# A third stream in prompt attention: the samples' paged-cache attention in units of 1024 tokens

## The chip, the cores and the metric

The kernel runs on one core of a Trainium2 chip. A core has a matrix engine (TensorE, in the profile PE, its weight loads PEld), a vector engine (VectorE, DVE), an activation engine (ScalarE, ACT), a general engine (GpSimd, POOL) and a sync engine (SyncE, SP) that issues most of the DMAs; GpSimd issues the gathers from the paged cache. Each engine works through its own queue in order and waits on semaphores. The metric is the device time of one execution in microseconds, as the median of several runs.

## The reference

One step of a two-layer decoder: a gated delta-rule mixer, a feed-forward part, latent attention, a feed-forward part again. It serves one prompt of 16 + 1024 tokens and 8 samples of one new token each, which all pass through the same matrices as 1048 columns. The change lies in the latent attention of the second layer. For a sample, with 8 heads, it is

```
q     = (rmsnorm(h @ w_q_a) @ w_q_b)            # per head: 128 plain, 64 rotary
q_lat = q_plain . w_uk                           # 256 latent numbers per head
s     = (q_lat . c_past + rope(q_pe) . k_past) * scale     # 4096 cached tokens
p     = softmax([s, s_new])                      # s_new: the token itself
o     = (p @ [c_past, c_new]) @ w_uv             # 128 per head
out   = concat(o) @ w_out
```

`c_past` (256 numbers a token) and `k_past` (64) lie in pages of 128 tokens, in an order that a page table gives. The prompt's 1040 tokens attend to one another causally; their keys and values are made from the latent with `w_uk` and `w_uv`. All arithmetic is float32.

## The kernel before

Tensors are kept with channels on partitions and tokens as columns, in three chunks (280, 384, 384); the samples are the first 8 columns of the first chunk. A float32 product is made of three products of rounded halves (`mm3`, lines 226 to 229), so most lines of the profile read L227, L228, L229 and are told apart by their tiles. Some products stay plain float32, which TensorE makes in two passes; a trace counts both.

`merge` (line 834) is what sets the order: it takes several generators, each of which yields a position before its next piece, and always runs the one whose position is lowest. A scheduler behind the kernel then orders each engine's queue by those priorities and by its own view of when operands are ready. The attention part of the second layer is three stages.

- Prompt attention, lines 1226 to 1441. `attend` goes through 8 heads of 9 query blocks: scores (`sc`, lines 1348 to 1384), softmax, the weights turned (`ptr`, `pT`) and multiplied with the values (`po`). `heads_in` makes queries (`qps`), keys (`knps`), rotary queries and values (`vps`) of the next head, just under a head earlier. Here also the samples' queries of the head are carried to the latent (`ukt`, `pq`). All of these but the scores use two PSUM buffers, `mtile` (line 98); a PSUM tile is free again when ScalarE or VectorE has copied it out.
- The samples' cache, `cache_unit` (line 1464): 16 units of 2048 tokens, two for a sample. GpSimd gathers two latent tiles (`cg`) and a rotary tile (`krt`). TensorE turns them (`dkt`, `dct`) through three PSUM buffers of their own; ScalarE and VectorE copy the result (`cT`, `krT`). The scores `dscr` are 8 x 4 products that each use 32 columns of the array, so four of them can run side by side. The value products `pv` are made in the same way.
- Beside the units, from position 0.05 to 1.0, the output projection of the prompt (`outp`, line 300, tile `psop`), without the samples' 8 columns; the units take positions 0 to CA = 0.4. `join` (line 1541) then merges the four key groups and the new token, carries the result through `w_uv` (`dov`) and makes the samples' own output projection (`dop`, line 1600; turned by `dopt`, line 1606), whose weights it loads a second time.

The lines of the latent scores:

```
for j in range(4):
    PE.matmul(sc[32 * j:32 * j + 32, :], ql[:, k, b, :], cT[:, j, :], start=(k == 0), stop=False,
              tile_position=(0, 32 * j))
```

Of the kernel before, what the change touches and what calls it, by code (L numbers as in the profile page):

```python
# [11 lines left out]
F32 = mybir.dt.float32  # L12
F32R = mybir.dt.float32r
# [7 lines left out]
P = 128  # L21
D = 1024
# [22 lines left out]
CA = 0.4  # L45
# [10 lines left out]
PTB = 4  # L56
# [5 lines left out]
def tile_step(ctx: ExitStack, tc: tile.TileContext, I, O, stop=None):  # L62
# [54 lines left out]
    # per-channel vectors as columns  # L117
# [56 lines left out]
    with tc.tile_pool(name="init", bufs=2, reuse_waits="tile") as ip, \  # L174
# [19 lines left out]
        # tokens to channel-major, normalised  # L194
# [40 lines left out]
    def stat(pp, aps, n, dst, dim):  # L235
        """dst[p, t] = (sum over channels / dim + eps)^-0.5 on every partition."""
# [10 lines left out]
    def boundary(pp, wide, c, wname, split=True, halves=False, store=False):  # L247
        """x <- x + acc * rstd * w for one chunk, kept in acc and, as halves, in xh and xl; the old x is in them or in x_d."""
# [99 lines left out]
    # ------------------------------------------------------------------ layer A mixer  # L348
# [38 lines left out]
    # previous conv rows of the samples, channel-major  # L387
# [9 lines left out]
    def gates():  # L397
# [20 lines left out]
        # a and b columns  # L418
# [40 lines left out]
        # cumulative decay  # L459
# [8 lines left out]
        # beta  # L468
# [91 lines left out]
    def chunks(h, p0, p1):  # L560
        """Everything of a head that does not need the running state."""
# [54 lines left out]
        # queries, meanwhile  # L616
# [21 lines left out]
        # last conv rows and sample rows  # L638
# [13 lines left out]
        # inverse of the 32-wide diagonal blocks by substitution: row k = 3 r + q of a block on partition (q, block)  # L652
# [81 lines left out]
    def recur(h, p0, p1):  # L734
        """The running state of a head, its outputs, and the samples."""
# [110 lines left out]
    def tail_a(p0, p1):  # L846
        """Out projection of the first heads while the last ones finish."""
# [14 lines left out]
    def tail_b(p0, p1):  # L862
        """The residual, channel-major."""
# [58 lines left out]
    # ------------------------------------------------------------------ gated conv feed-forward  # L922
# [170 lines left out]
    # ------------------------------------------------------------------ layer B: shared latent, attention  # L1093
# [8 lines left out]
    c_new = ukr.tile([NS, KVL], F32, name="c_new")  # L1102
    pgt = ukr.tile([P, NS], I32, name="pgt")
    for r in range(4):
        SP.dma_start(pgt[32 * r:32 * r + 32, :], I["page_table"].rearrange("b j -> j b"))
    rq = ukr.tile([P, 6], F32, name="rq")
    SP.dma_start(rq, I["c_rq"])
    idx = ukr.tile([P, 4, NS], I32, name="idx")
    idr = ukr.tile([P, 2, NS], I32, name="idr")
    for g in range(4):  # L1110
        V.tensor_scalar(idx[:, g, :], pgt, 16.0, rq[:, g:g + 1], op0=ALU.mult, op1=ALU.add)
    for g in range(2):
# [576 lines left out]
```

## Time and profile before

| | us |
|---|---|
| median of 3 runs | 3343.46 (3340.5 to 3355.22) |
| span of the profiled execution | 3338.6 |
| prompt attention, 1783 to 2173 | 390 |
| cache units beside the output projection, 2173 to 2412 | 239 |
| join beside the projection, 2412 to 2466 | 54 |
| rest of the projection, 2466 to 2514 | 48 |

The span runs from the first to the last instruction of one profiled execution; what its whole time was is not listed apart, and the median of the runs, taken without a profile, is 4.9 us above it. The page gives busy times by engine; since matmuls overlap one another, TensorE's real pace is read from the starts in the timeline. A wait is put down to what released it. Idle time of an engine counts only where TensorE or the end waits for it.

### The profile page before, as it was taken

How to read it: one execution, taken by the hardware profiler on the slowest of the kernel's cores; microseconds unless marked ns; L12 is line 12 of the kernel's file. 1: busy time of each engine (PE TensorE's matmuls, PEld its weight loads, DVE VectorE, ACT ScalarE, POOL GpSimd, SP SyncE). 2: the span in 40 equal slices, each digit the busy share in tenths (PEclk: the TensorE clock that was granted, in tenths of full speed). 3: DMA queues.
4: the chain of work that ended last, by engine and by line, in shares of the span. 5: the costliest groups of instructions: out<-in, count | busy, mean ns of one | idle time of the engine just before them, and what ended most of it. 6: DMA issues, size and time to landing. Idle time of an engine off the chain costs nothing.

```text
span 3338.6 us, 52527 instructions
## 1 busy us (share of the span) xinstructions
PE 3151.7 (94%) x20846; PEld 2874.7 (86%) x20846; DVE 2031.4 (61%) x4139; ACT 1255.9 (38%) x2541; POOL 860.2 (26%) x1013
## 2 busy tenths in 40 slices
PE   7999999999899999999888999999998999999997
PEld 6888888888699999999877888856677999999996
DVE  4877777766854555555666666544457455655556
ACT  4656555663432222222334444433224322222223
POOL 1432222210442223222431001112104323322322
PEclk9999999999899999999999999999999999999999
DMA  3222222236311111111121000255432111111111
GB/s 109 59 72 71 59 64 69 69 105 184 93 52 39 52 51 45 46 39 55 48 79 39 25 19 27 65 214 195 155 107 77 52 45 45 45 41 56 45 39 65
DMA packets 267649, 235.08 MB, mean 70 GB/s; under 512 B 57918, under 2 KB 246596, under 8 KB 263284
## 3 DMA queue, kind: packets, MB, share of 16 engines
q1 hardware_dynamic: 260224, 189.69, 19.7%
q0 software_dynamic: 6912, 41.95, 3.4%
q8 instruction: 164, 2.69, 0.3%
q14 instruction: 81, 0.66, 0.1%
q10 hardware_dynamic: 268, 0.09, 0.0%
HBM read 198.84 MB, written 33.40 MB: 70 GB/s over the span
## 4 chain that ended last, share of the span: by engine, by line
PE 77%; DVE 14%; DMA 3%; issue 3%; ACT 2%; POOL 1%; SPq 0%; ACTq 0%; DVEq 0%; POOLq 0%
PE fps L228 9%; PE fps L229 9%; PE fps L227 9%; PE fdn L228 5%; PE fdn L227 5%; PE fdn L229 5%; PE psu L227 2%; PE psu L229 2%; PE po L1409 2%; PE psu L228 2%; PE dscr L1494 2%; DVE acc L287 2%; DVE xs L660 1%; DVE tm L658 1%; PE psop L227 1%
## 5 line engine op out<-in xcount | busy, mean ns | idle before, releaser
L144 POOL TENSOR_TENSOR ws<-ws,vec 128x1024 f32<-128x1024 f32 (+1 forms) x127 | 247.6, 1950 | 433.4 <-DMA ws<-in_f_w_up_dram 173.2
L228 PE MATMUL fps<-xfl,wh 128*128 128x384 f32 (+1 forms) x1056 | 343.7, 326 | 8.3 <-POOL xfl L295 8.3
L227 PE MATMUL fps<-xfh,wh 128*128 128x384 f32 (+1 forms) x1056 | 341.7, 324 | 8.0 <-ACT xfh L293 7.0
L228 PE MATMUL fps<-xbl,wh 128*128 128x384 f32 (+1 forms) x1056 | 342.5, 324 | 6.1 <-POOL xbl L295 6.1
L229 PE MATMUL fps<-xfh,wl 128*128 128x384 f32 (+1 forms) x1056 | 342.4, 324 | 0.0
L227 PE MATMUL fps<-xbh,wh 128*128 128x384 f32 (+1 forms) x1056 | 340.6, 323 | 1.1 <-ACT xbh L293 0.5
L229 PE MATMUL fps<-xbh,wl 128*128 128x384 f32 (+1 forms) x1056 | 340.2, 322 | 0.0
L966 DVE TENSOR_TENSOR fu<-fps,RS 128x384 f32<-128x384 f32 x176 | 98.1, 557 | 386.7 <-PE fps L229 386.2
L151 ACT CAST wh<-ws 128x1024 fp32r<-128x1024 f32 (+1 forms) x144 | 148.0, 1028 | 488.1 <-PE fps L228 374.0
L227 PE MATMUL fdn<-gh,dh 128*128 128x384 f32 (+1 forms) x960 | 315.8, 329 | 0.0
L228 PE MATMUL fdn<-gl,dh 128*128 128x384 f32 (+1 forms) x960 | 311.9, 325 | 0.0
L229 PE MATMUL fdn<-gh,dl 128*128 128x384 f32 (+1 forms) x960 | 309.0, 322 | 0.0
L1044 DVE TENSOR_TENSOR acc<-acc,fdn 128x384 f32<-128x384 f32 (+1 forms) x432 | 216.9, 515 | 108.5 <-PE fdn L229 107.7
L227 PE MATMUL psu<-xah,wh 128*128 128x384 f32 (+1 forms) x768 | 261.2, 340 | 11.3 <-ACT u L533 7.0
L228 PE MATMUL psu<-xal,wh 128*128 128x384 f32 (+1 forms) x768 | 259.1, 337 | 0.4 <-DVE xal L223 0.4
L229 PE MATMUL psu<-xah,wl 128*128 128x384 f32 (+1 forms) x768 | 258.7, 337 | 0.7 <-DVE wl L152 0.7
L975 DVE SCALAR_TENSOR_TENSOR fy<-fu,fcv,fy 128x1064 f32<-128x1064 f32 x176 | 238.6, 1358 | 7.5 <-ACT fy L973 7.3
L152 DVE TENSOR_TENSOR wl<-ws,wh 128x1024 fp32r<-128x1024 f32 (+1 forms) x144 | 173.7, 1206 | 70.3 <-ACT wh L151 70.1
L228 PEld LDWEIGHTS fps<-xfl,wh 128*128 128x128 f32 x1056 | 200.8, 190 | 10.7 <-POOL xfl L295 10.5
L227 PEld LDWEIGHTS fps<-xfh,wh 128*128 128x128 f32 x1056 | 200.4, 190 | 9.4 <-ACT xfh L293 7.9
L228 PEld LDWEIGHTS fps<-xbl,wh 128*128 128x128 f32 x1056 | 199.6, 189 | 8.0 <-POOL xbl L295 7.7
L229 PEld LDWEIGHTS fps<-xfh,wl 128*128 128x128 f32 x1056 | 200.8, 190 | 0.4
(963 smaller groups left out, 7857.1 us busy)
## 6 DMA issues: line engine op xcount, KB each, us to landing
ws<-in_f_w_up_dram SPq DMA_DIRECT2D x88, 512.0 KB
ds<-in_f_w_down_dram SPq DMA_DIRECT2D x44, 512.0 KB
ws<-in_a_w_in_dram SPq DMA_DIRECT2D x32, 512.0 KB
xt<-in_x_prompt_dram SPq DMA_DIRECT2D x16, 512.0 KB
of<-og_d SPq DMA_DIRECT2D x32, 192.0 KB
xr<-x_d SPq DMA_DIRECT2D x16, 384.0 KB
GC<-gcd SPq DMA_DIRECT2D x24, 174.0 KB
Ss<-in_state_delta_S_dram SPq DMA_DIRECT2D x8, 512.0 KB
```

Source lines behind the costliest of these rows:

```text
L144: G.tensor_tensor(st, st, bc(fo, [P, kt, m]), op=ALU.mult)
L151: A.copy(hi, st)
L152: V.tensor_tensor(lo, st, hi, op=ALU.subtract)
L227: PE.matmul(ps, wh, ah, start=start, stop=False)
L228: PE.matmul(ps, wh, al, start=False, stop=False)
L229: PE.matmul(ps, wl, ah, start=False, stop=stop)
L287: V.scalar_tensor_tensor(a_[:, k + j, :], a_[:, k + j, :], vc(wname, k + j), res[j], op0=ALU.mult, op1=ALU.add)
L966: V.tensor_tensor(u[:, 18 + t0:18 + t0 + n], ps[:, :n], RS[:, t0:t0 + n], op=ALU.mult)
L975: V.scalar_tensor_tensor(y, u[:, j:j + LW], fcv[:, l, j, tl:tl + 1], y, op0=ALU.mult, op1=ALU.add)
L1044: V.tensor_tensor(acc[c][:, m, :], acc[c][:, m, :], ps[:, :n], op=ALU.add)
L1409: PE.matmul(po[:, :nq], vt[:kk, kb, P * (h % 2):P * (h % 2) + P], pT[:kk, j, :nq], start=(kb == 0), stop=(kb == i))
L1494: PE.matmul(sc[32 * j:32 * j + 32, :], ql[:, k, b, :], cT[:, j, :], start=(k == 0), stop=False, tile_position=(0, 32 * j))
```

## The change

The cache stage is gone as a stage. Prompt attention now has a third and a fourth stream, the samples' queries (`sample_queries`) and their cache (`cache_all`, positions 0.25 to 7.3 of the 8 heads). A unit is 1024 tokens: one latent gather, one rotary gather, half the columns in every product. Its transposes use the two buffers of `mtile`; its scores and value products share one PSUM bank, `halves`. The samples' queries are made for all heads at once from `w_q_b` in float32, no longer taken from the prompt's query tiles. Rings are shorter: softmax weights 2 for 3, their turned form 3 for 4, query tiles 2 for 3, rotary queries 3 for two heads for 4, values in three tiles of one head instead of two of two, the results `po` in one bank. The query norm takes the place of an earlier one (RQ = RS). After the join the samples' heads go to `og_d` beside the prompt's, and the output projection, now alone, takes all 1048 columns; `dop` and `dopt` are gone.

In the diff only the core is shown; of the old functions what is removed is in the listing above, of the new ones the main lines stand.

```diff
-PTB = 4
+PTB = 3
+PB = 2
+C0 = 0.25
+C1 = 7.3
...
-        opp = e2.enter_context(tc.tile_pool(name="ato", bufs=2, space=PSUM, reuse_waits="tile"))
+        opp = e2.enter_context(tc.tile_pool(name="ato", bufs=1, space=PSUM, reuse_waits="tile"))
+        dpp = e2.enter_context(tc.tile_pool(name="dps", bufs=1, space=PSUM, reuse_waits="tile"))
+        dc = e2.enter_context(tc.tile_pool(name="dc", bufs=1, reuse_waits="tile"))
+        cpg = e2.enter_context(tc.tile_pool(name="dcp", bufs=2, reuse_waits="tile"))
+        po4 = opp.tile([P, 4, C], F32, name="po")
+        halves = dpp.tile([P, 2, 256], F32, name="scpv")
...
-            return sp.tile([P, 384], F32, tag=nm, name=nm, bufs=3 if nm == "qu" else 2)
+            return sp.tile([P, 384], F32, tag=nm, name=nm, bufs=2 if nm == "qu" else 1)
...
-                pt = mtile("ukt")
-                for k in range(2):
-                    PE.transpose(pt[:, P * k:P * k + P], st[:, 3 + k, :], ident)
-                hd["ukT"] = sp.tile([P, 256], F32, tag="ukT", name="ukT", bufs=2)
-                A.copy(hd["ukT"], pt[:, :256])
...
-                        at[h + j]["qr"] = ap.tile([P, T], F32R, tag=f"qr{j}", name=f"qr{j}")
+                        at[h + j]["qr"] = ap.tile([P, T], F32R, tag="qr", name=f"qr{j}", bufs=3)
...
-                if c == 0:
-                    pq = mtile("pq")
-                    for k in range(2):
-                        PE.matmul(pq[:, NS * k:NS * k + NS], hd["ukT"][:, P * k:P * k + P], u[:, 0:NS], start=True, stop=True)
-                    V.tensor_copy(ql[:, :, :, h], pq[:, :2 * NS].rearrange("p (k s) -> p k s", k=2))
...
-                pp = sp.tile([C, NP], F32, tag="P", name="P")
+                pp = sp.tile([C, NP], F32, tag="P", name="P", bufs=PB)
...
-                        ot["po"] = opp.tile([P, C], F32, tag="o", name="po")
+                        ot["n"] = (ot.get("n", 0) + 1) % 4
+                        ot["po"] = po4[:, ot["n"], :]
...
-        cpg = e2.enter_context(tc.tile_pool(name="dcp", bufs=4, reuse_waits="tile"))
-        trp = e2.enter_context(tc.tile_pool(name="dtr", bufs=3, space=PSUM, reuse_waits="tile"))
...
+        def sample_queries():
+            yield -0.86
+            ps = halves[:, 0, :]
+            for a in range(2):
+                t = big("wq8")[:, :12 * P].rearrange("p (k h m) -> p k h m", k=3, h=4)
+                for k in range(3):
+                    SP.dma_start(t[:, k], wq[:, k, 4 * a:4 * a + 4, 0:128])
+                yield -0.6 + 0.1 * a
+                for h in range(4):
+                    o = NS * (4 * a + h)
+                    for k in range(3):
+                        PE.matmul(ps[:, o:o + NS], t[:, k, h, :], qa8[:, k, :], start=(k == 0), stop=(k == 2))
+            t = big("wr8")[:, :12 * P].rearrange("p (k m) -> p k m", k=3)
+            for k in range(3):
+                SP.dma_start(t[:, k, :].rearrange("p (h m) -> p h m", h=H), wq[:, k, :, 128:192])
+            yield -0.35
...
+            t = big("uk8").rearrange("p (k m) -> p k m", k=2)
+            SP.dma_start(t, I["kv_w_uk"].rearrange("(k p) h n -> p k (h n)", p=P))
...
+            pq = halves[:, 1, :]
+            for h in range(0, H, 4):
+                uT = cmat("ukT")
+                for i in range(2):
+                    yield -0.2 + 0.04 * (h + 2 * i)
+                    pt = mtile("ukt")
+                    for j in range(4):
+                        o = P * (h + 2 * i + j // 2)
+                        PE.transpose(pt[:, P * j:P * j + P], t[:, j % 2, o:o + P], ident)
...
+        def fetch(n):
+            if n < 4 * NS and n not in fetched:
+                b, g = divmod(n, 4)
+                cg = big("cg")
+                off = bass.IndirectOffsetOnAxis(ap=idx[:, g, b:b + 1], axis=0)
+                kr = cpg.tile([P, 8 * ROPE], F32, tag="kr", name="kr")
+                G.indirect_dma_start(kr, None, rrows, off)
+                G.indirect_dma_start(cg, None, crows, off)
+                fetched[n] = cg, kr
...
+        def cache_unit(n):
+            b, g = divmod(n, 4)
+            yield 0.0
+            fetch(n)
+            cg, kr = fetched.pop(n)
+            krT = cpg.tile([P, 512], F32, tag="krT", name="krT", bufs=1)
+            pt = mtile("dkt")
+            for i in range(4):
+                PE.transpose(pt[:, P * i:P * i + P], kr[:, P * i:P * i + P], ident)
+            A.copy(krT, pt)
+            cT = []
             for k in range(2):
...
+            yield 0.4
+            sc = halves[:, 0, :]
+            for k in range(2):
                 for j in range(4):
+                    PE.matmul(sc[32 * j:32 * j + 32, :], ql[:, k, b, :], cT[k][:, 2 * j:2 * j + 2, :], start=(k == 0), stop=False,
                               tile_position=(0, 32 * j))
...
+            yield 0.65
+            pT = cpg.tile([P, 2, P], F32, tag="dpT", name="dpT")
+            pt = mtile("dpt")
+            for c in range(2):
+                PE.transpose(pt[:, P * c:P * c + P], p[:, P * c:P * c + P], ident)
+            A.copy(pT, pt[:, :256].rearrange("p (a b) -> p a b", a=2))
+            yield 0.85
+            pv = halves[:, 1, :]
+            for c in range(2):
                 for j in range(4):
+                    o = KVL * key(j, c)
+                    PE.matmul(pv[32 * j:32 * j + 32, :], pT[:, c, 32 * j:32 * j + 32], cg[:, o:o + KVL],
+                              start=(c == 0), stop=(c == 1), tile_position=(0, 32 * j))
+            fetch(n + 2)
...
         def cache_all(p0, p1):
+            yield p0
+            fetch(0)
+            fetch(1)
+            for n in range(4 * NS):
+                for f in cache_unit(n):
+                    yield p0 + (p1 - p0) * (n + f) / (4 * NS)
+            yield p1 + 0.05
+            yield from join(p1 + 0.05, p1 + 0.5)
...
+                SP.dma_start(og_d[h][:, 0:NS], os_[:, h, :])
...
-            # their columns of the output projection
-                SP.dma_start(st, I["b_w_out"][0, P * h:P * h + P, :])
-                for i in range(2):
-                    PE.matmul(ps[i][:NS, :], os_[:, h, :], st[:, 512 * i:512 * i + 512], start=(h == 0), stop=(h == H - 1))
...
+        merge(attend(), *[heads_in(h, h - HA, h - HB) for h in range(H)], sample_queries(), cache_all(C0, C1))
+    emp.close()
...
-        merge(cache_all(0, CA), outp(I["b_w_out"][0], og_d, groups, ogp, 0.05, 1.0, True, NS, 6))
+        merge(outp(I["b_w_out"][0], og_d, groups, ogp, 0.0, 1.0, True, 0, 6))
```

Three places in TensorE's queue. First the scores of a cache unit before, in the middle of the stage; `dct` are turned keys, `dscr` the scores, and a wait names the engine waited for.

```order
L1488 MATMUL dct__23719<-ident,cg 128x128 [waits Activation_49]
L1488 MATMUL dct__23719<-ident,cg 128x128 x3
L1494 MATMUL dscr<-cT,ql 32x512
L1494 MATMUL dscr<-cT,ql 32x512 [waits DVE_49]
L1494 MATMUL dscr<-cT,ql 32x512 [waits Activation_49]
L1488 MATMUL dct__23730<-ident,cg 128x128 [waits PE_49]
L1494 MATMUL dscr<-cT,ql 32x512 [waits DVE_49]
L1488 MATMUL dct__23730<-ident,cg 128x128 x3
L1488 MATMUL dct__23736<-ident,cg 128x128 [waits PE_49]
L1488 MATMUL dct__23736<-ident,cg 128x128 x3
L1488 MATMUL dct__23742<-ident,cg 128x128 [waits PE_49]
```

The four products of the first latent half each wait for a copy of their own, and a transpose stands before the last one.

Now the same place of a unit after the change; the scores are written to `scpv`, `qps` are queries of the next head, `ptr` turned weights of the prompt's attention.

```order
L229 MATMUL qps<-qah,wh 128x280
L230 MATMUL qps<-qal,wh 128x280
L231 MATMUL qps<-qah,wl 128x280
L1546 MATMUL scpv<-cT,ql 32x256 x6
L1546 MATMUL scpv<-cT,ql 32x256 [waits DVE_49]
L1546 MATMUL scpv<-cT,ql 32x256
L1550 MATMUL scpv<-krT,qr_s 32x256 x4
L1390 MATMUL ptr<-ident,P 116x116 [waits PE_49]
L1390 MATMUL ptr<-ident,P 116x116
```

Six of the eight latent products stand together behind a group of queries; two more follow behind one wait, then the four rotary ones.

Last the start of attention after the change, in head 0: `wr` is the rotary query weights of the samples, `uk` the key weights that `ukt` turns, and the wait at the end is for the landing of a DMA.

```order
L1475 MATMUL scpv<-qa_17476,wr_18399 128x8 x9
L229 MATMUL sc<-knh,qnh 116x348 [waits Activation_49]
L230 MATMUL sc<-knl,qnh 116x348
L231 MATMUL sc<-knh,qnl 116x348 [waits Pool_49]
L1356 MATMUL sc<-kTh,qr_18272 116x348
L1357 MATMUL sc<-kTl,qr_18272 116x348
L229 MATMUL sc<-knh,qnh 116x464 [waits PE_49,Activation_49]
L230 MATMUL sc<-knl,qnh 116x464
L231 MATMUL sc<-knh,qnl 116x464
L1356 MATMUL sc<-kTh,qr_18272 116x464
L1357 MATMUL sc<-kTl,qr_18272 116x464
L1498 MATMUL ukt<-ident,uk_18465 128x128 [waits DMAHW0_49]
```

Between the last reading of the rotary weights and the first of the key weights stand ten score products of head 0. Nothing of this stood there before.

## Rows read from the trace of the kernel before

**Rows 1.** The page: span, and busy time of the engines

```profile
span 3338.6 us, 52527 instructions
PE 3151.7 (94%) x20846; PEld 2874.7 (86%) x20846; DVE 2031.4 (61%) x4139; ACT 1255.9 (38%) x2541; POOL 860.2 (26%) x1013
```

**Rows 2.** The page: the chain that ended last, by engine

```profile
PE 77%; DVE 14%; DMA 3%; issue 3%; ACT 2%; POOL 1%; SPq 0%; ACTq 0%; DVEq 0%; POOLq 0%
```

**Rows 3.** Stages: us; PE, PEld, DVE, ACT, POOL busy (x); clock; DMA share; GB/s

```profile
1783.00:2173.00 390.00, 373.37 (x2440) 313.46 (x2438) 238.65 (x662) 173.90 (x425) 41.95 (x42) 1.00 0.13 39
2173.00:2412.00 239.00, 234.70 (x1788) 142.16 (x1789) 108.53 (x222) 74.96 (x155) 39.84 (x42) 0.99 0.53 192
2412.00:2440.00 28.00, 28.00 (x190) 24.08 (x189) 11.41 (x41) 3.44 (x9) 0.10 (x1) 0.81 0.08 22
2440.00:2466.00 26.00, 23.93 (x78) 9.20 (x76) 7.82 (x12) 4.28 (x6) 2.12 (x3) 0.95 0.61 193
2466.00:2514.00 48.00, 45.46 (x280) 42.55 (x280) 36.08 (x59) 18.61 (x28) 3.80 (x2) 1.00 0.28 79
```

**Rows 4.** Timeline of a cache unit, TensorE: start, us, instructions

```profile
2326.39 1.93 PE L1517 MATMUL pv<-cg,dpT 128*32 128x256 f32 x32
2328.26 0.44 PE L1477 MATMUL dkt<-ident,krt 128*128 128x128 f32 x2
2328.53 0.60 PE L1488 MATMUL dct__23701<-ident,cg 128*128 128x128 f32 x4
2328.97 0.60 PE L1488 MATMUL dct__23707<-ident,cg 128*128 128x128 f32 x4
...
2330.58 1.35 PE L1494 MATMUL dscr<-cT,ql 128*32 128x512 f32 x6
2331.87 0.33 PE L1488 MATMUL dct__23730<-ident,cg 128*128 128x128 f32 x1
...
2333.10 0.55 PE L1488 MATMUL dct__23730<-ident,cg 128*128 128x128 f32 x3
...
2334.97 1.90 PE L1494 MATMUL dscr<-cT,ql 128*32 128x512 f32 x8
2336.80 1.06 PE L1498 MATMUL dscr<-krT,qr_s 64*32 64x512 f32 x8
2337.80 0.45 PE L227 MATMUL psop<-ogh,wx 128*128 128x384 f32 x1
...
2342.96 0.44 PE L1477 MATMUL dkt<-ident,krt 128*128 128x128 f32 x2
```

**Rows 5.** Groups by line, 2412 to 2466 us: output projection of the samples

```profile
L1600 PE MATMUL dop<-wos,os 128*8 128x512 f32 x32 | 16.6, 652 | 2.1 <-DMA wos<-in_b_w_out_dram 2.0
...
L1606 PE MATMUL dopt<-ident,ys 8*128 8x8 f32 x8 | 0.8, 207 | 0.0
```

**Rows 6.** Groups by line, 1783 to 2173 us: samples' latent queries

```profile
L1289 PE MATMUL pq<-qu,ukT 128*128 128x8 f32 x32 | 4.5, 249 | 0.5 <-DVE qu L1279 0.5
```

**Rows 7.** Gathers of latents (line 1469), then of rotary keys (line 1472)

```profile
DMA to landing us min/median/max: 5.5/7.0/8.8
...
DMA to landing us min/median/max: 6.0/7.9/8.9
```

**Rows 8.** Stages as rows 3, of an earlier layer and of attention's start

```profile
200.00:700.00 500.00, 459.29 (x3620) 423.51 (x3619) 372.38 (x1145) 295.18 (x819) 140.28 (x220) 0.97 0.26 69
1783.00:1830.00 47.00, 39.12 (x252) 33.63 (x251) 30.13 (x79) 22.49 (x57) 7.99 (x8) 1.00 0.18 53
```

**Rows 9.** Timeline of the same unit, copies of turned keys

```profile
2329.22 0.59 ACT L1492 COPY cT<-dct__23701 128x512 f32<-128x512 f32 x1 [2.88 <-PE dct__23701 L1488]
...
2329.60 0.69 DVE L1490 COPY cT<-dct__23707 128x512 f32<-128x512 f32 x1
```

**Rows 10.** Waits in attention: TensorE for copies, total us, times, longest

```profile
PEld vps L1325 <- ACT vt L1328: 8.4, 5, 1.8
...
PEld qps L227 <- DVE qu L1279: 3.4, 6, 1.0
```

More of the change, by code (lines that the diff above doesn't have):

```diff
@@ L44 @@
 PAGE = 128
-CA = 0.4
 CA0 = 0.65
@@ L1102, in tile_step @@
     c_new = ukr.tile([NS, KVL], F32, name="c_new")
+    qa8 = ukr.tile([P, 3, NS], F32, name="qa8")
     pgt = ukr.tile([P, NS], I32, name="pgt")
@@ L1105, in tile_step @@
         SP.dma_start(pgt[32 * r:32 * r + 32, :], I["page_table"].rearrange("b j -> j b"))
-    rq = ukr.tile([P, 6], F32, name="rq")
+    rq = ukr.tile([P, 4], F32, name="rq")
     SP.dma_start(rq, I["c_rq"])
     idx = ukr.tile([P, 4, NS], I32, name="idx")
-    idr = ukr.tile([P, 2, NS], I32, name="idr")
     for g in range(4):
         V.tensor_scalar(idx[:, g, :], pgt, 16.0, rq[:, g:g + 1], op0=ALU.mult, op1=ALU.add)
-    for g in range(2):
-        V.tensor_scalar(idr[:, g, :], pgt, 8.0, rq[:, 4 + g:5 + g], op0=ALU.mult, op1=ALU.add)
     emp = ExitStack()
@@ L1315, in v_weights @@
                 hd["uv"] = uh, ul
-                vt = ap.tile([C, NCK, 256], F32, tag="vt", name="vt")
-                at[h]["vt"] = at[h + 1]["vt"] = vt
+                for j in range(2):
+                    at[h + j]["vt"] = ap.tile([C, NCK, P], F32, tag="vt", name="vt", bufs=3)
             def vals(kb):
@@ new lines, in fetch, with key @@
+        def fetch(n):
[7 more added lines that the diff above has]
+                fetched[n] = cg, kr
+        def key(j, c):
+            return 4 * (j // 2) + 2 * c + j % 2
@@ new lines, in cache_unit @@
+        def cache_unit(n):
[9 more added lines that the diff above has]
+            cT = []
+            for k in range(2):
+                t = cmat("cT")
+                cT.append(t)
+                for hf in range(2):
+                    yield 0.06 + 0.12 * k + 0.06 * hf
+                    pt = mtile("dct")
+                    for i in range(4):
+                        o = KVL * key(2 * hf + i // 2, i % 2) + P * k
+                        PE.transpose(pt[:, P * i:P * i + P], cg[:, o:o + P], ident)
+                    (V.tensor_copy if hf else A.copy)(t[:, 4 * hf:4 * hf + 4, :], pt.rearrange("p (a b) -> p a b", a=4))
+            yield 0.4
+            sc = halves[:, 0, :]
+            for k in range(2):
@@ L1507, in cache_unit @@
             A.activation(p, sc, AF.Exp, bias=nb, scale=SCALE, accum_out=ls)
-            pT = sp.tile([P, 4, P], F32, tag="dpT", name="dpT")
-            pt = dtr("dpt")
-            for i in range(4):
-                PE.transpose(pt[:, P * i:P * i + P], p[:, P * i:P * i + P], ident)
-            A.copy(pT, pt.rearrange("p (a b) -> p a b", a=4))
-            pv = pvp.tile([P, KVL], F32, tag="pv", name="pv")
-            for i in range(4):
-                for j in range(4):
-                    o = KVL * (2 * i + j % 2)
-                    PE.matmul(pv[32 * j:32 * j + 32, :], pT[:, i, 32 * j:32 * j + 32], cg[j // 2][:, o:o + KVL],
-                              start=(i == 0), stop=(i == 3), tile_position=(0, 32 * j))
@@ new lines, in join, with jtile, dtr @@
+        def join(p0, p1):
+            uv = big("uv").rearrange("p (k m) -> p k m", k=2)
+            SP.dma_start(uv, I["kv_w_uv"].rearrange("(k p) h v -> p k (h v)", p=P))
+            OS = big("OSa").rearrange("p (b r) -> p b r", b=NS)
+            SP.dma_start(OS, os_d)
+            scr, used = cmat("jscr").rearrange("p a b -> p (a b)"), [0]
+            def jtile(*shape):
+                n = math.prod(shape[1:])
+                o = used[0]
+                used[0] += n
+                v = scr[:shape[0], o:o + n]
+                if len(shape) == 3:
+                    v = v.rearrange("p (a b) -> p a b", b=shape[2])
+                if len(shape) == 4:
+                    v = v.rearrange("p (a b c) -> p a b c", b=shape[2], c=shape[3])
+                return v
+            def dtr(nm):
+                return mtile(nm)
+            yield p0
```

180 lines of the change are left out of this document (82 added, 98 removed).

## The prediction

> **What bounds the kernel now.** I read the page first: TensorE is busy for 94% of a span of 3338.6 us [rows 1], and the chain of waits spends 77% of the span on it, 14% on VectorE and 3% on DMA [rows 2]. So time is won where TensorE's own time shrinks or where it stands still. Then I cut the stretch that the change touches into stages [rows 3]: prompt attention 390 us, the samples' cache units with the first part of the output projection 239 us, the samples' join 28 and 26 us, the rest of the projection 48 us: 731 us together, 22% of the span. TensorE is idle for 16.6 us of the first stage and 4.3 us of the second. The reader is to see that there is little idle time to fill: a third stream laid over attention cannot hide there, its TensorE time is added to attention's. What counts is whether the same work takes less TensorE time in the new form.
>
> The third view is the timeline of one cache unit of 2048 keys [rows 4], a pitch of 14.70 us. Read by starts, which is the time that TensorE gives to each part: four transposes 0.44; scores of the first latent half 2.52 (one transpose of 0.11 in it), of the second 1.83, rotary scores 1.00; products with the values 1.87. The rows differ in one thing. The value products are 32 instructions of 256 columns, in 8 rounds of four that run side by side, 0.234 us a round. The rotary scores are 2 rounds of 512 columns, 0.50 each, the same rate. The latent scores are also 2 rounds for each half and should take 1.00, but they take 2.41 and 1.83: the four do not start together. The order shows why: the second, third and fourth each wait for a copy of turned keys (by VectorE or ScalarE), and a transpose is put between them.
>
> **The sum, part by part.**
>
> Scores. Before: 2.41 + 1.83 + 1.00 = 5.24 us a unit of 2048. After, a unit of 1024 has three groups of four at 256 columns, two rounds each: 3 x 2 x 0.234 = 1.40, so 2.80 for 2048, if the four run together. Saved 2.44 x 16 = 39 us. The new order has the four in one piece in 40 of 64 latent groups; 24 are cut, into 25 pieces too many, at a group's 0.47 each: 12 us given back (bounds 0, where a cut piece is hidden, and 25 if the pieces that wait for a copy inside a whole group fall apart too). Net minus 27.
>
> Transposes, value products and weight turns keep their columns: 640 key transposes and 64 of the weights in either kernel, 256 value products. Nothing is won or lost on them.
>
> The join. The samples' own output projection goes: 16.6 us of matmuls, 2.1 us of idle time before them, and the turn of its result 0.8 [rows 5], 19.5 us. The two stretches it lies in were granted 0.81 and 0.95 of the clock [rows 3], so part of them ran at the 1.2 GHz level: 28 x 0.19 + 26 x 0.05 = 6.6 us, which full-rate work does not pay (bounds 0 and 6.6; I take it all, since attention was granted 1.00 throughout). Minus 26. The rest of the join goes on, among attention's work. The 4.3 us of idle time of the cache stage goes with the stage: minus 4. In the projection 8 columns more in 192 matmuls are under 1 us.
>
> Sample queries. 36 products on 8 columns are new, two passes each; a pass of that shape took 4.5/32 = 0.14 us [rows 6]: plus 10. The 16 turns of the key weights and their 32 passes only move.
>
> Their start. Query weights, rotary weights and key weights come in one after the other through two buffers: a load waits until TensorE has read the tile before it, and TensorE's next read of it waits for the landing. No row shows such a landing on this queue; the nearest, a gather of 0.5 MB, landed after 6.0 to 8.9 us [rows 7]. Between the waits the order puts some 4 to 5 us of values and scores of head 0. Behind the waiting instruction stands all of head 0; the sync queue holds the next head's weights behind the loads. Bounds 0 and 20 us (three loads of 8.9 with nothing beside them, less the 7.9 that TensorE already idles there [rows 8]); I take plus 6, two waits of about 3.
>
> Handover. The projection now starts straight after the last head instead of beside a cache unit: the halves of the first head are cast once attention's room is free. Plus 3, from 0 to 6.
>
> Waits in the merged stage. Each unit of 1024 asks six times for one of the two buffers that attention also uses (192 new requests; attention makes 27 a head, 216). A buffer is filled in 0.44 us, its copy starts 0.25 us later and takes 0.59 on ScalarE or 0.69 on VectorE [rows 4, 9]; two buffers back to back so give one tile per 0.67 instead of 0.44, 0.23 us of waiting for each tile that has no other work before it. The order puts scores or value products between most of them; 28 pairs of tiles stand back to back. Attention's two largest such waits were 8.4 and 3.4 us [rows 10]. I take 0.5 us a unit, plus 16. Bounds: minus 8, if half of attention's idle time is filled, and plus 94, if all 408 tiles wait 0.23. The shorter rings (two softmax buffers for three, one rotary buffer for two) are in that range.
>
> Gathers are hidden. A tile is asked for when the unit two before it is done, about 17 us ahead at 14 us a unit, against 8.9 for a landing [rows 7]. On GpSimd the gather waits for the value products, and attention's query halves stand behind it; they are made most of a head ahead, which covers it. Without that cover it is one landing, 9 us, per head.
>
> Sum: -27 - 26 - 4 + 10 + 6 + 3 + 16 = -22 us against the profiled span of 3338.6, so 3316.6. The median of the runs shown, 3343.5, is 4.9 above that span for what lies around it: **3321 us**.
>
> **Two rules weighed.** The waits of attention on its copies are a few us [rows 10], with 216 tiles in 390 us. The Trainium skill, "Trainium Kernel Development and Optimization", Best Practices, says to mind PSUM pressure, since tiling TensorE speeds up the compute but not the evacuation. By that rule the faster scores only bring the copies to the fore, and the sum would be that of the first rival; by the rows, which give every tile some neighbouring work, it stays as above.
>
> Attention was granted 1.00 with 4% of it idle [rows 3]; the stage from 200 to 700 us, TensorE 92% busy, was granted 0.97 [rows 8]. The skill's "TensorE: Matmul & The Clock Gate", "A second HAM failure mode: psum-queue depth-cycling", says that small idle times between groups of matmuls can throw the clock back and forth. By it the merged stage would go the way of that other stage; this is the third rival.
>
> **Rivals.** First, the two buffers become the bound and the kernel is slower: each of the 192 new tiles waits 0.23 us (44) and each old tile, now behind a new one, half of it (25), 69 us instead of 16: +53 - 22 = +31, 3375 us. For it: two buffers where the cache stage had three, and the in-order queue that all three streams share. Against it: the order rarely puts two tiles back to back, and VectorE and ScalarE are 61% and 45% busy in attention, so they have room. It decides from 0.135 us of wait per tile (55 us) upwards; there it is 0.5% slower.
>
> Second, the gains are eaten and nothing is seen: the cut groups cost 25 instead of 12 and the start of the queries 10 instead of 6, 17 us less: 3338.
>
> Third, the clock: the merged stage, some 600 us, is granted 0.97: +18, 3339.
>
> Fourth, more than forecast: cut pieces are hidden, the start costs nothing and waits are as now: -12 - 6 - 16, 3287. For it speaks that a scheduler placed the pieces where TensorE had other work.
>
> That the change doesn't do what it says (the units bunched at one place) the order excludes: a unit stands about every 60 rows of TensorE's queue, from head 0 to head 7.
>
> **How the numbers follow.** Chances: forecast 0.50 (its own range 3306 to 3330), buffers 0.16, eaten 0.15, clock 0.05, more 0.14. The measurement can tell about 0.5%, that is below 3326.7 or above 3360.2. Faster: 0.45 of the forecast's 0.50, and 0.14: 0.59. Same: the rest of the forecast, eaten and clock, 0.25. Slower: the buffers, 0.16. The range of 8 in 10 leaves out the lower half of the fourth case and most of the first: 3290 to 3354.
>
> **What would show it.** Latent scores right: in the new timeline most groups of four 256-column matmuls start within a few hundredths of a microsecond, and a unit's scores take about 1.4 us by starts; wrong if they stay near 2.6. Join right: no matmul on the output weights outside the projection, and the projection granted 1.00. Query start: waits of TensorE on the sample weights' DMAs of 3 to 9 us in all at the head of attention. Buffers: TensorE's waits on copies of turned keys and of softmax weights add up to under 30 us; over 55 the first rival has it. Merged stage: about 600 us long, from the first key of head 0 to the first projection matmul (attention's 390, the units' 239 less some 40 of projection in it, less 31, plus 32, plus 11 of the join), and the projection about 100. A granted clock under 0.98 there is the third rival. The forecast falls if the merged stage exceeds 640 us.

## The result: slower by 0.6%, where 0.7% faster was forecast

The changed kernel took 3367.8 us (median of 9 runs, 3356.1 to 3380.6), the kernel before 3343.5 us beside it; the ratio is 1.0063, 95% interval 1.0039 to 1.0087. The forecast was 3321 with a range of 3290 to 3354.

The page of the changed kernel, the answer to [rows 1, 2]:

```profile
span 3374.8 us, 53697 instructions
PE 3179.3 (94%) x21262; PEld 2919.7 (87%) x21262; DVE 2042.9 (61%) x4290; ACT 1278.2 (38%) x2633; POOL 881.7 (26%) x1029
...
PE 76%; DVE 14%; DMA 3%; ACT 3%; issue 3%; POOL 1%; SPq 0%; ACTq 0%; DVEq 0%; POOLq 0%
```

TensorE is busy for 27.6 us more and the shares are as before: the page doesn't say where. The stages do. The windows below have the columns of [rows 3]: the head of the merged stage, its middle, its end, the projection, and the boundary (residual and norms, from the last projection matmul to the last norm matmul).

```profile
1799.50:1862.00 62.50, 59.84 (x347) 53.67 (x345) 32.70 (x94) 22.20 (x58) 12.37 (x12) 0.81 0.48 141
1862.00:2370.00 508.00, 502.86 (x3988) 369.77 (x3987) 297.77 (x893) 220.23 (x555) 86.42 (x88) 1.00 0.29 98
2370.00:2415.20 45.20, 43.40 (x236) 35.82 (x236) 17.27 (x53) 12.96 (x29) 0.00 (x0) 0.77 0.20 63
2415.20:2520.60 105.40, 96.91 (x578) 93.65 (x577) 43.16 (x77) 26.27 (x52) 5.69 (x3) 0.95 0.24 71
2520.60:2592.00 71.40, 47.01 (x207) 38.50 (x207) 54.59 (x67) 32.94 (x48) 28.19 (x18) 0.76 0.36 104
```

The boundary of the kernel before, same columns:

```profile
2513.20:2556.00 42.80, 32.19 (x168) 28.45 (x167) 35.84 (x39) 19.57 (x29) 25.82 (x15) 0.88 0.35 108
```

So the span divides into four. Up to the first key product the changed kernel is 15.9 us late (1799.5 against 1783.6 us). From there to the last projection matmul it takes 720.8 us instead of 729.4: the changed stages did win, 8.6 us. The boundary takes 71.3 instead of 42.6: 28.7 lost, in code that the change doesn't touch. The rest is 783.1 against 783.0. The sum is 36.1, the difference of the two spans 36.2.

Why the boundary grew, ScalarE's timeline shows (start, us, instruction, idle time before it and what ended it). After:

```profile
2507.69 0.84 ACT L259 ACTIVATE s<-acc 128x768 f32<-128x768 f32 x1
2520.66 1.58 ACT L259 ACTIVATE sq<-acc 128x768 f32<-128x768 f32 x2 [12.13 <-PE psop L231]
```

Before, the same instruction:

```profile
2472.49 0.85 ACT L257 ACTIVATE sq<-acc 128x768 f32<-128x768 f32 x1 [1.76 <-DVE acc L336]
```

The second square of the boundary's first chunk waited 12.1 us for the very last projection matmul, which is of another chunk. It has no use for that matmul's result; so it waits, I take it, for its scratch tile's place. In the kernel before the pool of the projection's operands was opened behind three pools of the sample cache, and the boundary's tiles later fell on the places of these. In the changed kernel these pools are in the attention stage, the projection's operands stand first, and the boundary's tiles fall on them. The trace holds no addresses; two runs below test this. The order of TensorE has no norm matmul among the projection's 576 any more, where the kernel before has three pairs, 60 to 175 matmuls ahead of the end. The residual loads on the sync queue wait in the same way:

```profile
SPq L277 <- DVE ogl L327: 14.3, 1, 14.3
SPq L277 <- PE psop L231: 12.3, 1, 12.3
```

### The profile page after: what moved, and what is told of

The parts are those of the page before. It is cut to its first block, busy times and chain, and to the rows that moved or that the text cites. A ratio compares the mean times of both kernels' runs of the same rounds, so it can differ in the third digit from the quotient of the medians.

```text
span 3374.8 us, 53697 instructions
## 1 busy us (share of the span) xinstructions
PE 3179.3 (94%) x21262; PEld 2919.7 (87%) x21262; DVE 2042.9 (61%) x4290; ACT 1278.2 (38%) x2633; POOL 881.7 (26%) x1029
## 4 chain that ended last, share of the span: by engine, by line
PE 76%; DVE 14%; DMA 3%; ACT 3%; issue 3%; POOL 1%; SPq 0%; ACTq 0%; DVEq 0%; POOLq 0%
PE fps L230 9%; PE fps L231 9%; PE fps L229 9%; PE fdn L230 5%; PE fdn L229 5%; PE fdn L231 4%; PE psu L229 2%; PE psu L231 2%; PE psu L230 2%; PE po L1405 2%; PE dct L1540 2%; DVE acc L289 2%; DVE tm L660 1%; PE scpv L1546 1%; PE psop L229 1%
## 5 line engine op out<-in xcount | busy, mean ns | idle before, releaser
L229 PEld LDWEIGHTS fps<-xbh,wh 128*128 128x128 f32 x1056 | 201.5, 191 | 11.8 <-ACT xbh L295 10.1
```

Source lines behind the costliest of these rows:

```text
L229: PE.matmul(ps, wh, ah, start=start, stop=False)
```

## The experiments

**Theories.** Cover: what was lost is the boundary running beside the projection, by where its tiles lie. Rival to it: the loss is the clock, or the first part of the program. Pieces: the scores won less than forecast because they are still cut. Clock: the passes on 8 sample columns pull TensorE to its lower level. Times by starts (from one TensorE start to the next) are sums over the records from the first key product to the last projection matmul.

**The same two kernels again** (no edit).

> The changed kernel once more. In its profile the first 1783 us of the program before the change, whose instructions stand in the same order in both kernels, took 15.9 us longer (first key product of the attention at 1799.5 us instead of 1783.6). If that is a chance of the single execution (its granted clock was at half level for 116 us of the first 1000 instead of 75), the first key product now stands anywhere between 1780 and 1800 us, and the stretches after it stay: 721 us to the last projection matmul, 71 us from there to the last norm matmul of the boundary. If the new kernel slows the first part by itself, it stands at 1799 us again, within 3 us.

> The kernel before, a second profile. Stretch by stretch, as the four profiles of the changed order so far have it: if the first part varies by chance, the first key product stands between 1779 and 1800 us and not at 1783.6; the stretches behind it repeat within 3 us: 729 us to the last projection matmul, 43 us to the last norm matmul of the boundary, 783 us to the end. If the first part is a property of each kernel, the key product stands at 1783.6 within 3 us.

Measured for the changed kernel: 3362.0 us, ratio 1.0052 (1.0034 to 1.0070); first key product at 1779.7 us, then 719.3, 69.6 and 783.3 us. For the kernel before: first key product at 1777.2, then 733.3, 42.4 and 782.8. The first part is chance: the first key products of the two profiles of the changed kernel stand 19.8 us apart, those of the two kernels stood 15.9 apart. The first 1000 us of these two profiles, the first and then the second, differ in the granted clock:

```profile
0.00:1000.00 1000.00, 896.79 (x6440) 823.00 (x6441) 708.35 (x1861) 536.39 (x1369) 273.47 (x389) 0.94 0.30 83
```

```profile
0.00:1000.00 1000.00, 899.80 (x6553) 824.93 (x6554) 714.47 (x1868) 544.23 (x1385) 282.42 (x398) 0.96 0.31 84
```

Over the twelve profiles of this study the first key product stands between 1777 and 1800 us, and up to the latents the order of instructions is the same in all. The stretches behind it repeat within 4 us. What is left is 9 to 14 us won in the changed stages and 27 to 29 lost in the boundary, 13 to 20 us in all; the two ratios make 17 and 21.

**Room below the projection's operands**, in the changed kernel:

```diff
     with ExitStack() as e2:
+        rm = e2.enter_context(tc.tile_pool(name="room", bufs=1, reuse_waits="tile"))
+        G.memset(rm.tile([P, 6144], F32, name="room")[:, 0:1], 0.0)
         ogp = e2.enter_context(tc.tile_pool(name="ogt", bufs=8, reuse_waits="tile"))
```

> The changed kernel with 24 KB a partition of unused room allocated below the projection's operands, nothing else. Cover theory: the boundary's scratch tiles then no longer lie where the projection's turned queries and weights lie, the boundary of the first chunk runs beside the last chunk's projection again as in the kernel before, and the 71.4 us from the last projection matmul to the last norm matmul of the boundary go back to about 43: 25 to 29 us off, about 3340 us, no slower than the kernel before. Rival, the clock or the residual loads make that stretch long: the room changes nothing, within 5 us of the changed kernel. Second rival, the first part of the program is what costs: the room changes nothing either, and the first key product is late by 16 us.

**The opposite edit** in the kernel before: the line that opens `ogt` goes ahead of the one that opens `dc`.

> The kernel before, with the pool of the projection's operands opened ahead of the pools of the sample cache instead of behind two of them, nothing else. Cover theory: now the boundary's scratch tiles lie over the projection's operands here too, the boundary waits for the last projection matmul, and the 42.6 us from that matmul to the last norm matmul grow to about 70: 25 to 29 us slower than the kernel before, ratio about 1.008. Rival: no change, ratio 1.000 within 0.002.

Measured: with room 3344.1 us, 0.9991 (0.9978 to 1.0004) of the kernel before, so 20 to 24 us off the changed kernel; the kernel before with its pools swapped 3364.1 us, 1.0051 (1.0032 to 1.0071). The boundary's window with room, and then in the swapped kernel with the wait that now appears there too:

```profile
2520.40:2561.00 40.60, 35.03 (x164) 29.49 (x162) 36.08 (x39) 17.11 (x26) 28.54 (x17) 0.76 0.34 99
```

```profile
2513.20:2584.00 70.80, 46.97 (x211) 38.70 (x211) 54.81 (x68) 33.22 (x49) 28.21 (x18) 0.73 0.36 105
```

```profile
2513.47 1.58 ACT L257 ACTIVATE sq<-acc 128x768 f32<-128x768 f32 x2 [11.90 <-PE psop L229]
```

Both ways the boundary moves by 28 to 31 us, and a pool opened or moved is all that was changed. The cover theory holds. (The swapped line stood behind three pools, not two as the expectation says.) Its net is smaller, 17 us by the ratio of the swapped kernel: its stretch up to the last projection matmul fell by 6.9 (729.4 to 722.5), since the norms and turns that left the projection no longer cost there. One thing stays open: behind the boundary the kernels with the room take 785 to 788 us, all the others 782 to 784.

**Whole pieces.** In the changed kernel with room, and then in the kernel before, the products of a group are issued so that the first waits for the last copy:

```diff
-            for k in range(2):
-                for j in range(4):
+            for k in (1, 0):
+                for j in (2, 3, 0, 1):
```

```diff
-                for j in range(4):
+                for j in (3, 2, 1, 0):
```

> The changed kernel with the unused room, and the eight latent score products of a cache unit issued in reverse, so that the first of them waits for the last copy of turned keys: the order then has all eight and the four rotary ones in one piece in each of the 32 units, instead of 59 pieces of latent scores. Theory: each cut costs a round of 0.23 to 0.47 us and the entry and exit of a piece; a unit's scores go from 1.98 us by starts to about 1.5, and the kernel is 12 to 16 us faster than with the room alone. Rival: the wait for the last copy comes out as idle time ahead of the first product, 0.3 to 0.5 us a unit, and the kernel gains nothing, within 4 us.

> The kernel before, with the four score products of each latent half issued in reverse, so that the first of them waits for the last copy of turned keys and the others wait for nothing. Theory: in the kernel before the four of a group start 0.215 us apart because each waits for its own copy, 63.6 us for 32 groups; side by side a group takes two rounds of about 0.47 and its exit, 1.0 us, 32 us in all: 25 to 32 us faster, about 3315 us, without any merging. Rival: the wait for the last copy comes out as idle time of TensorE, about 1 us a group, and nothing is gained, within 5 us.

Measured: 0.9965 (0.9949 to 0.9981) and **0.9935 (0.9920 to 0.9949)**, 3335.6 and 3325.0 us. By the median the fastest kernel of the study that does the whole work is the old one with one loop turned round. Latent scores by starts fell from 45.3 to 32.0 us in the merged form and from 63.6 to 31.9 in the old one; the stretch to the last projection matmul fell from 722.5 to 710.6 and from 729.4 to 697.9. First a cut unit of the changed kernel (TensorE's timeline), then a whole one of the same kernel, then the unit in the old kernel turned round, to be read against [rows 4]:

```profile
1906.85 0.62 PE L1546 MATMUL scpv<-cT,ql 128*32 128x256 f32 x2
1907.40 0.66 PE L1540 MATMUL dct<-ident,cg 128*128 128x128 f32 x4
1907.99 1.05 PE L1546 MATMUL scpv<-cT,ql 128*32 128x256 f32 x10
...
1909.31 0.63 PE L1546 MATMUL scpv<-cT,ql 128*32 128x256 f32 x4
1909.87 0.64 PE L1550 MATMUL scpv<-krT,qr_s 64*32 64x256 f32 x8
```

```profile
2000.14 1.07 PE L1546 MATMUL scpv<-cT,ql 128*32 128x256 f32 x16
2001.14 0.64 PE L1550 MATMUL scpv<-krT,qr_s 64*32 64x256 f32 x8
2001.71 0.42 PE L1390 MATMUL ptr<-ident,P 116*116 116x116 f32 x2
```

```profile
2335.00 1.06 PE L1494 MATMUL dscr<-cT,ql 128*32 128x512 f32 x8
2335.99 0.66 PE L1488 MATMUL dct__23742<-ident,cg 128*128 128x128 f32 x4
...
2337.89 1.06 PE L1494 MATMUL dscr<-cT,ql 128*32 128x512 f32 x8
2338.89 1.06 PE L1498 MATMUL dscr<-krT,qr_s 64*32 64x512 f32 x8
2339.88 0.44 PE L229 MATMUL psop<-ogh,wx 128*128 128x384 f32 x1
```

The same eight passes that took 1.83 us in one piece [rows 4] take 0.99. So a group that the order shows whole was not side by side. In the piece of [rows 4] the first two products start at 2334.97, the third at 2335.20 and the last at 2335.83, these two within 0.06 us of the end of a copy of turned keys, on ScalarE and then on VectorE:

```profile
2334.56 0.59 ACT L1492 COPY cT<-dct__23742 128x512 f32<-128x512 f32 x1 [0.23 <-PE dct__23742 L1488]
2335.08 0.69 DVE L1490 COPY cT<-dct__23748 128x512 f32<-128x512 f32 x1 [0.27 <-PE dct__23748 L1488]
2335.83 0.14 PEld L1494 LDWEIGHTS dscr<-cT,ql 128*32 128x32 f32 x2 [0.49 <-DVE cT L1490]
```

With the loop turned round the first waits for the last copy, and all four go together. The rival fails in the old kernel: the weight loads of its scores wait for the copies as below (total us, times, longest), 0.2 us a group instead of the 1 us that would have eaten the gain; in the kernel before it was 10.3 us.

```profile
PEld dscr L1494 <- DVE cT L1490: 6.2, 30, 0.3
```

The whole kernels won less than was expected. In the merged form 12 to 16 us were expected; the stretch won 11.9, the ratios make 9, and their intervals touch. In the old one 25 to 32 were expected; the stretch won 31.5, but the ratio makes 22. Of the difference 6.4 us went in its boundary (49.0 us instead of 42.6), which no run explains.

**Queries turned round**, and then **the join in pieces** besides. The edits in short:

```diff
-                        PE.matmul(ps[:, o:o + NS], t[:, k, h, :], qa8[:, k, :], start=(k == 0), stop=(k == 2))
+                    PE.matmul(q[:NS, :], qa8[:, k, :], t[:, k, :], start=(k == 0), stop=(k == 2))
+                    PE.transpose(ps[:, o:o + NS], q8[:, P * h:P * h + P], ident[:NS, :NS])
```

```diff
-C1 = 7.3
+C1 = 7.0
+                    yield p0 + (p1 - p0) * (0.6 + 0.2 * k + 0.025 * b)
+                yield p1 + 0.03 * h
```

> The changed kernel with room, with whole score pieces, and with the samples' queries turned round: the 8 sample columns are the fixed operand and 512 weight columns are streamed, 9 products instead of 36, and 12 small turns bring the result back. Clock theory: the runs of 20 passes of 8 columns drop the granted clock to half at the head of attention (20 to 24 us in each of the five profiles of the changed order, from 2 to 3 us after the first such run); without them the stretch is granted 1.00 there, about 10 to 12 us won, and the passes themselves fall from 12.3 us to an estimated 5 or 6: 15 to 18 us faster than with whole pieces alone. Rival: the half clock there comes of something else (the waits for the loads, the 32 passes of the key weights): it stays, and only the passes are won, 4 to 7 us.

> As the one before, with the join of the samples begun 0.3 of a head earlier and its products on 8 columns issued in pieces between attention's, instead of 36 and 32 passes in a row. Clock theory: those runs drop the clock to half for 17 to 20 us at the end of attention (in the kernel before 14 us); in pieces they don't, and 8 to 10 us are won. Rival: the half clock stays with the pieces, and the change is within 3 us of the run before.

Measured: 0.9954 for both (0.9936 to 0.9972, and 0.9937 to 0.9972), against 0.9965 for whole pieces alone: no difference. The gains of both theories failed to come; of the join in pieces the rival came out. The 18 wide passes took 10.3 us by starts, 0.43 in the median, where I had estimated half of that; the 72 narrow ones had taken 12.9, most of it at the lower level. And the lower level stayed, at the head (20.5 us of it instead of 27.3) and in the join (20.5 in pieces). (The expectation's five profiles of the changed order were four.) At the head it fell at other places, though. With the queries turned round (the windows before and after each fall):

```profile
1797.00:1803.00 6.00, 4.25 (x27) 3.77 (x25) 1.57 (x3) 2.53 (x6) 4.31 (x5) 1.00 0.50 148
1803.00:1810.00 7.00, 5.73 (x17) 3.23 (x18) 1.30 (x4) 0.00 (x0) 0.53 (x1) 0.51 1.05 312
...
1820.00:1827.00 7.00, 5.49 (x30) 3.46 (x28) 5.78 (x19) 2.27 (x5) 2.26 (x2) 0.99 0.45 151
1827.00:1841.00 14.00, 12.04 (x51) 11.07 (x51) 7.86 (x25) 4.43 (x13) 1.00 (x1) 0.52 0.15 39
```

The first fall stands ahead of the first wide pass (1804.3 us), in a wait of TensorE for its weights of 2.4 us; the second stands in a wait of 2.8 us for a copy of attention. In the changed kernel, with 20 narrow passes in a row just before the fall, TensorE had been busy for 3.7 of the 4 us before it, and with room for all 4. So this run doesn't clear the narrow passes: the fall behind a run of them is gone, and two behind idle time stand in its place. Idle time alone does not settle it either: at the head of the kernel before TensorE was busy for 10.60 of 15 us (1800 to 1815) and was granted 1.00.

**Left out.** Two kernels on top of whole pieces: one without the samples' queries (`ql` and `qr_s` set to zero), one without the join's products `dol` and `dov` (VectorE fills their place).

> The changed kernel with room and whole pieces, and without the samples' queries: their three loads, 36 products and 16 turns with 32 passes are left out, the tiles that they fill are set to zero; the cache units follow as before. With the queries the merged stage has 16.3 us of their passes, 3 us of turns and 24 us at half clock at the head of attention, and 710.6 us from the first key product to the last projection product. If the half clock comes from the queries' work in any form, it goes, and 16 + 3 + about 12 = 31 us are won: about 680. If it comes from the cache stream's start itself (gathers, the loads of the first heads beside them), 20 us at half clock stay and 16 to 20 us are won: about 692.

> The changed kernel with room and whole pieces, and without the join's two sets of products on 8 columns (36 products of the weighted sums and 32 of the value weights); VectorE fills the samples' columns from the loaded tiles instead. With them the end of the merged stage has 12 us of these passes and 17 us at half clock. If these passes are what the clock falls for, the stretch is granted 1.00 up to the projection and 12 less the full-rate part plus 9 of the other work are won: 710.6 goes to about 698. If the thin end of attention (short of the cache stream) is the reason, the half clock stays and only 8 us are won: about 703.

Measured: 0.9887 (0.9861 to 0.9912) and 0.9895 (0.9869 to 0.9920). Without the join's products the stretch went from 710.6 to 693.8 us, 16.8 for 12.1 us of passes, and more than either figure of the expectation (698 and 703). The end of attention with them (whole pieces), then without:

```profile
2350.00:2358.00 8.00, 8.00 (x53) 6.32 (x53) 4.57 (x16) 1.83 (x4) 0.00 (x0) 1.00 0.00 1
2358.00:2375.00 17.00, 17.00 (x72) 15.21 (x71) 1.92 (x7) 2.02 (x4) 0.00 (x0) 0.50 0.06 13
```

```profile
2340.00:2360.00 20.00, 20.00 (x160) 13.64 (x153) 12.46 (x43) 8.32 (x23) 0.00 (x0) 1.00 0.39 129
2360.00:2380.00 20.00, 19.09 (x128) 15.03 (x129) 10.48 (x35) 8.84 (x22) 0.00 (x0) 1.00 0.26 72
```

In the join the lower level goes with these passes: the eleven profiles that have them show 13.6 to 30.7 us of it there, the one without them none. Without the queries the head keeps 10.2 of its 27.3 us at the lower level:

```profile
1782.00:1803.00 21.00, 18.25 (x116) 16.19 (x114) 11.64 (x28) 9.44 (x24) 7.93 (x8) 1.00 0.63 185
1803.00:1815.00 12.00, 9.94 (x44) 8.81 (x44) 10.68 (x29) 3.90 (x11) 2.00 (x2) 0.57 0.25 80
```

Here too it fell behind idle time (a wait of 1.7 us for attention's rotary queries). So most of the head's lower level goes with the queries' work; whether by its passes or by the waits that it brings stays open. The stretch fell by 12.7 only, less than either theory said, but the join of that execution had 30.7 us at the lower level instead of 17.1; by the ratios this kernel is 26 us faster than whole pieces alone, between the two theories.

## Why the prediction was wrong

**What was left out of the sum.** It has no term for the boundary, and its list of signs ended with the projection. The lengths came out (the merged stage 616 us for "about 600", the projection 105 for "about 100"). Other signs did not: a unit's scores took 1.98 us in the mean, not 1.4; the merged stage was granted 0.96, and the projection 0.95, not 1.00. But the larger loss stood in the stage behind them. I read what the order of instructions moved and not what the memory behind it did: a pool that is opened first in a stage is where the next stage's tiles land. With room the kernel is level with the one before (0.9991), so this step alone turned "no change" into "slower by 0.6%"; that it is level and not 22 us faster is the sum's own fault.

**The sum itself** said 22 us won; the stages won 8.6, and 4.5 of that were norms and turns that had gone to the boundary. TensorE's time by starts, before and after, in us:

```
scores (latent and rotary)              79.5 ->  63.5   -16.0   forecast -27
samples' projection (dop, dopt)         18.7 ->   0.0   -18.7   forecast -19.5
sample queries and weight turns          4.7 ->  19.3   +14.6   forecast +10, and +6 for the start
attention's own (sc po ptr vps qps
  knps scx)                            380.8 -> 402.6   +21.7   forecast +16 (waits)
products with the cache values          30.2 ->  34.2    +4.0   forecast 0
turns of cached keys (dct dkt)          79.4 ->  72.4    -7.0   forecast 0
projection (psop)                      108.0 -> 105.2    -2.9   forecast 0
norms and turns of the next stage        5.1 ->   0.6    -4.5   not in the forecast (fpst 1.2, st_ps 3.3)
the whole stretch, at the lower level   16.9 ->  51.3
```

- Scores, mis-sized by 11. One unit gave 5.24 us [rows 4]; the mean of 16 is 4.97, 4.3 us less to win. A whole unit takes 1.57 by starts (1.00 and 0.57), not 1.40, since each piece has an exit: 5.4. The cuts cost 13.3 (45.3 - 32.0), for 12 forecast: that term was right.
- Join. The passes went as forecast. The 6.6 us for its clock did not come: only 3.5 us of the `dop` passes had run at the lower level; another 8.0 were `dol` and `dov`, which stay. They took it into attention, 20.5 us of it instead of 13.7, and the projection has 10.3 us more, which began in a wait of 5.2 us for a weight.
- Start of the queries. The waits on their weights were 1.7 us (the first row below), not 6, below the 3 to 9 that I named. The lower level at 1821 us, 23.9 us of it, was not in the sum, and it is more than the wait was:

```profile
PE scpv L1467 <- DMA wq<-in_b_w_q_b_dram: 1.7, 2, 1.1
```

```profile
1799.00:1821.00 22.00, 20.20 (x136) 18.43 (x133) 12.81 (x32) 9.55 (x24) 6.91 (x7) 1.00 0.61 173
1821.00:1844.00 23.00, 23.00 (x96) 20.94 (x97) 13.04 (x44) 4.57 (x13) 1.98 (x2) 0.50 0.49 142
2374.00:2384.00 10.00, 10.00 (x60) 7.35 (x59) 6.45 (x24) 2.90 (x9) 0.00 (x0) 1.00 0.17 62
2384.00:2404.00 20.00, 20.00 (x85) 18.17 (x85) 2.82 (x8) 2.96 (x5) 0.00 (x0) 0.50 0.05 11
```

- Waits in the merged stage, the term with the wrong sign. Forecast 16 more than before; TensorE's idle time fell. It is 9.6 us in the merged stage (by the first three windows of the changed kernel above), where the stages that it replaces had 23.0 [rows 3]; behind attention's own products it is 8.3 instead of 15.8. All waits of the merged stage add up to 8.4 us, 6.7 without those on weights, and none is on a gather; the largest on copies are the first two rows below, and the weight loads wait for the copies of turned keys as in the third and fourth:

```profile
PE ptr L1390 <- DVE P L1378: 1.1, 1, 1.1
PE dct L1540 <- DVE cT L1541: 1.1, 2, 0.9
```

```profile
PEld dct L1540 <- DVE cT L1541: 3.0, 5, 1.2
...
PEld dct L1540 <- ACT krT L1530: 2.9, 10, 0.5
```

The first rival, two buffers as the bound, is refuted by the same rows.

- Attention's own products, whose slowing the sum put at nothing: with idle time taken off they went from 365.0 to 394.3 us, 29.3 more. They spent 21.7 us at the lower level, about half of it lost, and the other 18 us were lost at the full one. A small part of these is the change between streams: after a value product of attention the next one starts 0.11 us later, a product that is one of four side by side 0.20, at 28 places some 3 us. I have not tested the rest.
- The third rival. The merged stage was granted 0.96 (its three windows weighted by length), under the 0.98 that I had set for it, and 34 us more at the lower level in the whole stretch cost about 17, its price of 18. But not by its mechanism. The Trainium skill, "TensorE: Matmul & The Clock Gate", "A second HAM failure mode: psum-queue depth-cycling", has small idle times between groups as the cause. Here the middle, where the streams alternate, was granted 1.00 over 508 us, and in the join the clock fell at 2384.2 us behind 10.00 of 10.00 us busy. At the head, at 1821.0, TensorE had been idle for 0.6 us of the 6 before; only the fall in the projection, at 2469.5, came in a longer wait, of 5.2 us.

No rival describes what came: it has a part of the second (gains eaten), the price of the third, and a stage that no rival looked at. That the page of the first profile also showed 15.9 us lost ahead of attention was chance.

## What to carry to other kernels

When a stage is merged or a pool moved, look at what the next stage's tiles will lie on, and at the instructions of the next stage that used to stand among the last matmuls of this one: if they are gone from there, that cover has a price. A group of products that can run side by side did so here only when its first waited for the last thing that any of them needs; turning a loop round brought 0.65% where merging two stages brought nothing. Ask first whether the gain of a large change can be had where the work stands.

## What the runs showed of the hardware

- Products on 32 columns each, side by side: a piece of the changed kernel's latent scores takes 0.55 to 0.57 us to the next start if it has up to four products (one round, each product in two passes) and 0.98 to 1.00 if it has five to eight (two rounds); one piece of 59 took 0.82. One product alone costs as much as four.
- The granted clock fell to 0.50, the 1.2 GHz level, 1.5 to 5.2 us after the first of the join's passes on 8 columns (`dol` at 2382.5, fall at 2384.2 us in the changed kernel; 2425.6 and 2429.2 before), with TensorE busy without a gap by the records in ten profiles of eleven. With the passes split into pieces of 4 to 18 it still fell; without them it did not.
- A pass of 512 columns whose product has 8 rows takes 0.43 us by starts in the median (`dop` before, and the queries turned round); eight such passes of the scores, in two rounds of four side by side, take 0.99 to 1.00.
- One order of instructions, twelve profiles: the way to the first key product varies by 22 us, with 61 to 123 us at the lower level in the first 1000.
